# Spread modulation steps and a written-out VectorE order in the product FFNs of a diffusion backbone

## The chip, the cores and the metric

The kernel runs on one core of a Trainium2 chip. Five engines of that core take part: TensorE (PE) multiplies matrices into PSUM banks; VectorE (DVE) and ScalarE (ACT) do the element-wise work; GpSimd (POOL) and SyncE (SP) issue DMA transfers. Each engine works through its own list of instructions in order; semaphores tie the lists together. The metric is the device time of one execution in microseconds (us), the median of several runs.

## The reference, cut to what matters

The model is a trunk of two layers over 512 latent tokens and 256 context tokens, 1024 wide, in fp32. Each layer is a half-step SwiGLU FFN, a mixer (a gated convolution in layer 0, attention in layer 1), and a second half-step FFN. Each sub-layer has its own modulation vectors (shift, scale and gate), computed from a conditioning vector:

```python
for i in range(DEPTH):
    m_lat = (silu_c @ ada_w[i] + ada_b[i]).reshape(b, N_SUBLAYERS, N_MOD, 1, d)
    m_ctx = (silu_cc @ ada_w[i] + ada_b[i]).reshape(N_SUBLAYERS, N_MOD, 1, d)
    h = norm_modulate(x_lat, norm_g[i, 0], m_lat[:, 0, 0], m_lat[:, 0, 1])
    x_lat = x_lat + MACARON_WEIGHT * m_lat[:, 0, 2] * swiglu(h, ffn_w_in[i, 0], ffn_w_out[i, 0])
    ...                                # the same for the context, then the mixer, then the second FFN

def swiglu(h, w_in, w_out):
    gate, up = jnp.split(h @ w_in, 2, axis=-1)
    return (jax.nn.silu(gate) * up) @ w_out
```

## The kernel before, in words

**Stages.** The four sub-layers of layer 0 and 1 that matter here are called f00 (first FFN), c01 (the convolution), f02 (second FFN) and f10 (first FFN of layer 1); attention and the last FFN follow. All values are fp32. PE takes them as pairs: a high part (ACT copies the number into the rounded type, names ending in h or plain gh, tT3h, w) and a low part (DVE subtracts the high part from the number, names ending in l). One block of a product is then three matmuls: lines 808, 809 and 810. The helper `split` issues the copy (line 179) and the subtraction (line 180).

**Products.** The input half of an FFN (1024 to 2 x 2816) is computed in 22 chunks c of 128 gate and 128 up columns. Apart from two or three first chunks, which are multiplied plainly ("direct"), each chunk is done with seven products M1 to M7 in place of eight, on sums of token halves (T1 to T4, made once a stage) and sums of weight blocks (S1 to S4, made on DVE from the loaded `raw` tiles, lines 347 and 356). A product is 12 matmuls of 128x384. Their order on PE is M1(c), M2(c), M7(c-1), M5(c), M6(c), M4(c-1), M3(c-1). M1, M6, M7 and M4 of a chunk add up in one PSUM bank, ps_A; M5 and M3 in another, ps_C; M2 is in ps_B. In between, the partial results are read out of the bank, and the next product may not write to it until that has been done:

- M1: ACT copies ps_A to g (line 1067); M2: DVE adds ps_B to it (1069).
- M5: ACT copies ps_C to c (line 1072); M6: ACT copies ps_A to a second g (1075).
- M7: DVE adds ps_A to c (line 1078). M4 writes the same bank, and waits for it.
- M4: DVE multiplies ps_A into the silu of g (line 1129). M3: DVE adds ps_C to the second g (line 1083), which gives c12; its silu and a product with c follow (lines 1134 and 1137).

Every four chunks (28 products, a "T block") an "out" phase multiplies what the gate gave with the output weights: 144 matmuls of 512 or 256 columns into ps_A and ps_C, whose results DVE adds to the tokens x (line 874). It begins right behind M3, so its second ps_C bank is the one that line 1083 has to empty.

**Weights.** SP loads `raw` tiles (512 KB) into five buffers. `w_fill` turns them into `w` tiles (eight buffers), sums first, then high and low parts. At a stage's end some weights of the next stage are made ahead ("held").

**Modulation.** The vectors of later sub-layers are computed on DVE while PE multiplies. A block loads a 128x512 tile `aw` of ada_w (256 KB, by POOL, line 495) and reduces it against the silu of the conditioning row `crow`, once for the latents and, where they are needed, once for the context (line 505: a reduce that writes `jk` or back to `aw`, and a short read of the accumulator). `ADA_BY` says how far each stage gets: f00 computes 6 vectors (192 reduces), f02 4 (128), f10 5 (96). `bg()`, called after each product, hands out as many as are due, none in the out phases.

**What sets the order.** SP's and PE's lists are in program order. DVE's and ACT's lists are set by a scheduler that goes by its own estimates; a modulation reduce may be moved anywhere that its data allow, apart from the first of a stage.

Of the kernel before, what the change touches and what calls it, by code (L numbers as in the profile page):

```python
# [38 lines left out]
ADA_BY = {"f00": 6, "f02": 10, "f10": 15}  # L39
ADA_DEPTH = {"f00": 3, "f02": 3, "f10": 3}  # L40
# [80 lines left out]
def backbone(ctx: ExitStack, tc: tile.TileContext, a: dict, out: bass.AP):  # L121
# [56 lines left out]
    def split(dsth, dstl, src):  # L178
        act.activation(dsth, src, AF.Copy)  # L179
        dve.tensor_tensor(out=dstl, in0=src, in1=dsth.bitcast(F32), op=ALU.subtract)  # L180
# [64 lines left out]
    def w_fill(most=1 << 30):  # L245

        end = state["next"] + most
        while state["next"] < min(len(stream), end):
            n = state["next"]
            event, where, k, make = stream[n]  # L250
# [6 lines left out]
            raw_fill()  # L257
            dst = place(n, where, k)
# [8 lines left out]

    def w_get(most=1 << 30):
        w_fill(max(most, state["used"] + 1 - state["next"]))
# [17 lines left out]
    def add_plain(raw, u, ks, where=None, event=None):  # L287
        def make(dh, dl):
            split(dh, dl, raw_tiles[raw][0][:, u, ks])
            raw_used(raw)  # L290
        stream.append((event, where, ks.stop - ks.start, make))
# [50 lines left out]
    def add_product(g, u, m):  # L342
# [6 lines left out]
        def make(dh, dl):  # L349
            if m == "M1":  # L350
                split(dh, dl, quad(0))
            elif m == "M2":
                split(dh, dl, quad(1))
            elif m == "M5":
                sub(0, 0, 2)
                dve.tensor_tensor(out=quad(2), in0=quad(2), in1=quad(3), op=ALU.add)
                split(dh, dl, quad(2))
            elif m == "M6":
                sub(2, 3, 0)
                split(dh, dl, quad(2))  # L360
            elif m == "M7":
                split(dh, dl, quad(0))
            elif m == "M4":
                split(dh, dl, quad(3))
            else:
                sub(1, 1, 2)
                split(dh, dl, quad(1))
# [3 lines left out]
        stream.append((None, None, 4, make))  # L371
# [118 lines left out]
    def ada_next(n):  # L490

        if n < ahead["limit"]:
            i, m, k, c0 = ada_blocks[n]
            w = ada_loaded[n] = ahead["pool"].tile([P, HALF], F32, name=f"aw{i}_{m}_{k}_{c0}", tag="aw", bufs=ADA_DEPTH[ahead["key"]])
            nc.gpsimd.dma_start(w, a["ada_t"][i, m, k, :, c0 : c0 + HALF])  # L495

    def ada_block(n, v, nv):

        i, m, k, c0 = ada_blocks[n]
# [4 lines left out]
        if pinned[0]:  # L506
            tc.keep_in_program_order(ins)
        pinned[0] = False
        if v == nv - 1:
            ada_loaded.pop(n)  # L510
            ada_next(n + ADA_DEPTH[ahead["key"]])
# [13 lines left out]
    pinned = [False]  # L525
# [20 lines left out]
    def bg_start(key, pool, first, last):  # L546

        pace.update(n=0, done=0, first=first, last=last, tasks=ada_tasks.pop(key, []))
        pace["steps"] = len(pace["tasks"])
# [4 lines left out]
    def bg():  # L554
# [4 lines left out]
        if pace["n"] == pace["first"] - 6:  # L559
            rows_load(0)  # L560
# [1240 lines left out]
```

## Time and profile before

| what | value |
|---|---|
| time, median of 3 runs (lowest, highest) | 2502.87 us (2501.15, 2503.94) |
| time of the profiled execution | 2499.04 us |
| its span | 2497.3 us |
| mean granted clock of PE | 0.994 |
| f00, c01, f02, f10 begin at | 32, 584.8, 836.4, 1352.8 us |
| attention, last FFN begin at | about 1877, 2107 us |
| f02: out phase 0, first T block behind it | 875.22 to 891.90, 891.90 to 955.26 us |

The span is the time from the first to the last instruction; 1.7 us of the profiled execution lie outside it. The profiled execution is 3.8 us faster than the median of the runs. In the profile's parts, "busy" of PE counts overlapping matmuls once, and a matmul's duration is longer than the distance to the next one, since they are pipelined: 0.34 us long, one every 0.176 us, for 384 columns. DVE's durations too overlap a little: back-to-back subtractions of 128x512 last 0.69 us and start 0.60 us apart.

### The profile page before, as it was taken

How to read it: one execution, taken by the hardware profiler on the slowest of the kernel's cores; microseconds unless marked ns; L12 is line 12 of the kernel's file. 1: busy time of each engine (PE TensorE's matmuls, PEld its weight loads, DVE VectorE, ACT ScalarE, POOL GpSimd, SP SyncE). 2: the span in 40 equal slices, each digit the busy share in tenths (PEclk: the TensorE clock that was granted, in tenths of full speed). 3: DMA queues.
4: the chain of work that ended last, by engine and by line, in shares of the span. 5: the costliest groups of instructions: out<-in, count | busy, mean ns of one | idle time of the engine just before them, and what ended most of it. 6: DMA issues, size and time to landing. Idle time of an engine off the chain costs nothing.

```text
span 2497.3 us, 35662 instructions
## 1 busy us (share of the span) xinstructions
PE 2436.3 (98%) x13632; PEld 2263.3 (91%) x13632; DVE 1897.2 (76%) x3758; ACT 1094.2 (44%) x2016; POOL 135.1 (5%) x254
## 2 busy tenths in 40 slices
PE   6999999999999999999999999999999999999998
PEld 3889999999999999999999999899997889888887
DVE  4699999878968899996667989866668887544443
ACT  4443343355525643433435534244346775433233
POOL 0011111000000001110000021200000000000000
PEclk9999999999999999999999999999999999999999
DMA  7333543330213034533221155522231101332221
GB/s 276 110 125 116 165 155 129 110 110 26 76 51 117 28 106 148 161 123 102 85 74 49 67 172 167 183 79 68 68 110 60 43 18 60 102 101 93 96 82 34
DMA packets 92155, 252.53 MB, mean 101 GB/s; under 512 B 10192, under 2 KB 19536, under 8 KB 91984
## 3 DMA queue, kind: packets, MB, share of 16 engines
q1 hardware_dynamic: 71072, 183.00, 22.3%
q0 software_dynamic: 20064, 66.08, 8.2%
q8 instruction: 107, 1.75, 0.3%
q10 hardware_dynamic: 848, 1.18, 0.1%
q14 instruction: 64, 0.52, 0.1%
HBM read 248.11 MB, written 2.10 MB: 100 GB/s over the span
## 4 chain that ended last, share of the span: by engine, by line
PE 74%; issue 11%; DVE 8%; ACT 2%; POOL 2%; DMA 2%; SPq 0%; POOLq 0%; DVEq 0%; ACTq 0%
PE ps_A L809 14%; PE ps_A L808 14%; PE ps_A L810 14%; PE ps_C L808 7%; PE ps_C L810 7%; PE ps_C L809 7%; POOL aw L495 2%; PE ps_B L810 2%; PE ps_B L809 2%; PE ps_B L808 2%; DVE w L180 2%; DVE aw L505 1%; DVE jk L505 1%; PE ps_T L1481 1%; DVE x L874 0%
## 5 line engine op out<-in xcount | busy, mean ns | idle before, releaser
L179 ACT ACTIVATE w<-raw 128x512 fp32r<-128x512 f32 (+2 forms) x810 | 491.5, 618 | 752.4 <-PE ps_A L810 460.3
L180 DVE TENSOR_TENSOR w<-raw,w 128x512 fp32r<-128x512 f32 (+2 forms) x810 | 541.2, 677 | 183.9 <-ACT w L179 175.2
L809 PE MATMUL ps_A<-gl,w 128*128 128x512 f32 (+2 forms) x624 | 212.6, 341 | 0.4 <-DVE gl L180 0.4
L808 PE MATMUL ps_A<-gh,w 128*128 128x512 f32 (+2 forms) x624 | 212.1, 340 | 0.1
L810 PE MATMUL ps_A<-gh,w 128*128 128x512 f32 (+2 forms) x624 | 212.0, 340 | 0.0
L495 POOL DMA_DIRECT2D aw<-in_ada_t x240 | 129.6, 540 | 1130.5 <-DVE mods L505 1109.6
L874 DVE SCALAR_TENSOR_TENSOR x<-ps_A,gat,x 128x512 f32<-128x512 f32 (+1 forms) x192 | 118.6, 619 | 79.7 <-PE ps_A L810 79.5
L808 PE MATMUL ps_C<-gh,w 128*128 128x512 f32 (+1 forms) x472 | 166.6, 353 | 9.1 <-DVE g L1083 8.8
L809 PE MATMUL ps_C<-gl,w 128*128 128x512 f32 (+1 forms) x472 | 165.9, 352 | 0.0
L810 PE MATMUL ps_C<-gh,w 128*128 128x512 f32 (+1 forms) x472 | 165.7, 351 | 0.0
L809 PE MATMUL ps_A<-hl,w 128*128 128x512 f32 (+1 forms) x424 | 162.6, 384 | 2.4 <-DVE hl L668 2.4
L808 PE MATMUL ps_A<-h,w 128*128 128x512 f32 (+1 forms) x424 | 162.2, 382 | 1.0 <-DVE x L874 1.0
L810 PE MATMUL ps_A<-h,w 128*128 128x512 f32 (+1 forms) x424 | 162.1, 382 | 0.0
L347 DVE TENSOR_TENSOR raw<-raw,raw 128x512 f32<-128x512 f32 x204 | 139.5, 687 | 8.8 <-DMA raw<-in_ffn_w_in 6.3
L809 PEld LDWEIGHTS ps_A<-gl,w 128*128 128x128 f32 x624 | 118.6, 190 | 16.0 <-DVE gl L180 1.9
L808 PEld LDWEIGHTS ps_A<-gh,w 128*128 128x128 f32 x624 | 118.5, 190 | 15.2 <-ACT gh L179 1.0
L810 PEld LDWEIGHTS ps_A<-gh,w 128*128 128x128 f32 x624 | 118.6, 190 | 12.9
L874 DVE SCALAR_TENSOR_TENSOR x<-ps_C,gat,x 128x512 f32<-128x512 f32 (+1 forms) x136 | 87.7, 645 | 52.0 <-PE ps_C L810 51.8
L808 PEld LDWEIGHTS ps_C<-gh,w 128*128 128x128 f32 x472 | 90.0, 191 | 22.5 <-issue 11.3
L808 PE MATMUL ps_A<-tB11h,w 128*128 128x384 f32 x312 | 106.9, 343 | 3.0 <-ACT tB11h L763 2.9
L809 PE MATMUL ps_A<-tB11l,w 128*128 128x384 f32 x312 | 106.1, 340 | 0.3 <-DVE tB11l L765 0.3
L810 PE MATMUL ps_A<-tB11h,w 128*128 128x384 f32 x312 | 105.7, 339 | 0.0
(426 smaller groups left out, 6623.9 us busy)
## 6 DMA issues: line engine op xcount, KB each, us to landing
raw<-in_ffn_w_in SPq DMA_DIRECT2D x174, 512.0 KB, 3.7
aw<-in_ada_t POOLq DMA_DIRECT2D x240, 256.0 KB, 3.2
raw<-in_ffn_w_out SPq DMA_DIRECT2D x76, 512.0 KB, 3.9
raw<-in_conv_w_in SPq DMA_DIRECT2D x24, 512.0 KB, 3.7
ada<-in_ada_w SPq DMA_DIRECT2D x27, 256.0 KB, 6.0
raw<-in_attn_w_qkv SPq DMA_DIRECT2D x12, 512.0 KB, 4.8
raw<-in_ada_w SPq DMA_DIRECT2D x8, 512.0 KB, 5.2
raw<-in_conv_w_out SPq DMA_DIRECT2D x8, 512.0 KB, 3.7
```

Of the source, the lines that this page charges most:

```text
L179: act.activation(dsth, src, AF.Copy)
L180: dve.tensor_tensor(out=dstl, in0=src, in1=dsth.bitcast(F32), op=ALU.subtract)
L347: dve.tensor_tensor(out=quad(o), in0=quad(x), in1=quad(y), op=ALU.subtract)
L495: nc.gpsimd.dma_start(w, a["ada_t"][i, m, k, :, c0 : c0 + HALF])
L505: ins = dve.tensor_tensor_reduce(out=junk, in0=w, in1=ahead["rows"][:, v], scale=1.0, scalar=out if c0 else ada_b[:, i, m, k : k + 1], op0 ...
L808: pe.matmul(ps, wh, xh, start=first, stop=False, **kw)
L809: pe.matmul(ps, wh, xl, start=False, stop=False, **kw)
L810: pe.matmul(ps, wl, xh, start=False, stop=last, **kw)
L874: dve.scalar_tensor_tensor(out=x, in0=p[:, o - off : o - off + w], scalar=gat[:, m, v : v + 1], in1=x, op0=ALU.mult, op1=ALU.add)
L1481: pe.transpose(pt[:, c, :], pr[:, (c0 + c) * P : (c0 + c + 1) * P], ident)
```

## The change

- **The modulation is dealt out otherwise.** f00 computes 5 vectors (160 reduces), c01 one (32 reduces); f02 and f10 the same as before. Steps are due after each product (weight 1) and also inside the out phases (weights 6 and 3 in turn, 27 in all). Every reduce is held at its place in the program. In c01 the `aw` tiles have two buffers, elsewhere three.
- **The `aw` loads are issued by SP** instead of POOL, at the next call of `bg()` after their buffer came free.
- **DVE's order is written out** from the last direct chunk to the last out phase of f00, f02 and f10 (`chain()`, `unchain()`): what the program says first is first on DVE. A product's reading of PSUM comes first, then the modulation due, then the low parts that were put off (`late_parts`, emptied by `flush`), then the sums for the next weight (`pre()`). In the chain `w_get` makes only the weight that is needed, and `w_fill` runs after a product. ACT's order remains the scheduler's.

What is computed and PE's order of matmuls are the same; the number of reduces in all too (416). Line numbers move: 179 and 180 become 209 and 205 (the helper), 347 and 356 become 392 and 403, 505 becomes 554, 874 becomes 920, 1067 to 1083 become 1126 (copy of M1), 1128 (sum of M2), 1131 (copy of M5), 1134 (copy of M6), 1137 (sum of M7) and 1142 (sum of M3); 1129 and 1137 of before become 1202 and 1213.

```diff
-ADA_BY = {"f00": 6, "f02": 10, "f10": 15}
-ADA_DEPTH = {"f00": 3, "f02": 3, "f10": 3}
+ADA_BY = {"f00": 5, "c01": 6, "f02": 10, "f10": 15}
+ADA_DEPTH = {"f00": 3, "c01": 2, "f02": 3, "f10": 3}
+OUT_WEIGHT = (6, 3)
...
+    def chain():
+        chained.append(ExitStack())
+        chained[0].enter_context(tc.manual_schedule(engines=CHAIN_ORDERED))
+        w_fill()
...
+    def flush():
+
+        for _ in range(len(late_parts)):
+            late_parts.pop(0)()
+        if chained:
+            raw_fill()
...
-    def split(dsth, dstl, src):
+    def split(dsth, dstl, src, then=None):
+
+        def low():
+            dve.tensor_tensor(out=dstl, in0=src, in1=dsth.bitcast(F32), op=ALU.subtract)
+            if then:
+                then()
+
         act.activation(dsth, src, AF.Copy)
-        dve.tensor_tensor(out=dstl, in0=src, in1=dsth.bitcast(F32), op=ALU.subtract)
+        if chained:
+            late_parts.append(low)
+        else:
+            low()
...
+    def w_ahead():
+
+        flush()
+        if state["next"] < len(stream):
+            pre, raw = stream[state["next"]][4:]
+            if all(r in raw_tiles for r in raw):
+                pre()
+
     def w_get(most=1 << 30):
-        w_fill(max(most, state["used"] + 1 - state["next"]))
+        flush()
+        w_fill(max(0 if chained else most, state["used"] + 1 - state["next"]))
+        flush()
...
-            nc.gpsimd.dma_start(w, a["ada_t"][i, m, k, :, c0 : c0 + HALF])
+            nc.sync.dma_start(w, a["ada_t"][i, m, k, :, c0 : c0 + HALF])
...
-        if pinned[0]:
-            tc.keep_in_program_order(ins)
-        pinned[0] = False
+        tc.keep_in_program_order(ins)
...
-            ada_next(n + ADA_DEPTH[ahead["key"]])
+            ada_freed.append(n + ADA_DEPTH[ahead["key"]])
...
+    def bg(at):
+
+        while ada_freed:
+            ada_next(ada_freed.pop(0))
...
-        span = pace["last"] - pace["first"] + 1
-        due = min(pace["steps"], -(-pace["steps"] * (pace["n"] - pace["first"] + 1) // span))
+        pace["now"] += pace["slots"].get(at, 0)
+        due = min(pace["steps"], -(-pace["steps"] * pace["now"] // pace["total"]))
         while pace["done"] < due:
             pace["tasks"][pace["done"]]()
             pace["done"] += 1
...
+            if m == "out":
+                if begin <= count <= end:
+                    slots.update({(count, 1 + q): OUT_WEIGHT[q % 2] for q in range(6)})
...
             w_done()
             if c == total - 1:
                 traced.add((key, m))
+            if chained:
+                w_fill()
...
                 product(c, m)
-                bg()
+                traced_products += 1
+                bg((traced_products, 0))
+                if chained:
+                    w_ahead()
...
             if n == steps[-1]:
                 free_order()
+                if key != "c01":
+                    chain()
```

**The end of a T block.** DVE's list at the end of f10's second T block, before (the trace has it from 1564 to 1574 us). L1129 is the product of M4, L1083 empties the ps_C bank of M3, L505 is a modulation reduce and its accumulator read, L180 a low part (w of a weight, gl of the gate's result):

```order
L180 TENSOR_TENSOR w_14784<-raw_14659,w_14784 128x512
L505 ISA aw_5_5_512_16045,mods_81<-aw_5_5_512_16045,crow_15126,mods_81 128x512
L505 ISA mods_81 128x1
L1129 TENSOR_TENSOR g_14543<-g_14543,ps_A 128x384
L180 TENSOR_TENSOR w_14807<-raw_14706,w_14807 128x512
L505 ISA aw_5_6_512_16073,mods_81<-aw_5_6_512_16073,crow_15126,mods_81 128x512
L505 ISA mods_81 128x1
L180 TENSOR_TENSOR gl_14339<-g_14543,gh_14337 128x384
L1083 TENSOR_TENSOR g_14626<-ps_C,g_14626 128x384
```

The changed kernel's DVE list at the same place, with the out phase's first evictions (L920) behind it:

```order
L1202 TENSOR_TENSOR g_14548<-g_14548,ps_A 128x384
L205 TENSOR_TENSOR w_14789<-raw_14696,w_14789 128x512
L205 TENSOR_TENSOR gl_14360<-g_14548,gh_14358 128x384
L1142 TENSOR_TENSOR g_14625<-ps_C,g_14625 128x384
L554 ISA aw_7_5_0_14714,mods_81<-aw_7_5_0_14714,crow_13413,packed 128x512
L554 ISA mods_81 128x1
L205 TENSOR_TENSOR w_14809<-raw_14696,w_14809 128x512
L1213 TENSOR_TENSOR g_14625<-g_14625,c_14607 128x384
L205 TENSOR_TENSOR gl_14360<-g_14625,gh_14358 128x384
L920 SCALAR_TENSOR_TENSOR x<-ps_C,gat,x 128x512
L920 SCALAR_TENSOR_TENSOR x<-ps_A,gat,x 128x512
```

The two reduces that stood between the product of M4 and the sum of M3, or just ahead of them, are gone from there; the one that is due after M3 stands behind its sum.

**The first T block of a stage, ACT.** In f02, just behind out phase 0, before: tT3h and tT4h are high parts of the token sums T3 and T4, the three PSUM copies are those of M5, M6 and the next chunk's M1, the rest are high parts of weights:

```order
L179 ACTIVATE tT3h<-fT_8157 128x768 x2
L179 ACTIVATE tT4h<-fT_8418 128x768
L179 ACTIVATE w_8320<-raw_7561 128x512
L179 ACTIVATE w_8324<-raw_8214 128x512
L179 ACTIVATE w_8375<-raw_8214 128x512
L179 ACTIVATE w_8378<-raw_7550 128x512
L179 ACTIVATE w_8381<-raw_8222 128x512
L1072 ACTIVATE c_8453<-ps_C 128x384
L1075 ACTIVATE g_8475<-ps_A 128x384
L1067 ACTIVATE g_8494<-ps_A 128x384
L179 ACTIVATE w_8434<-raw_8222 128x512
L179 ACTIVATE w_8438<-raw_7561 128x512
```

The same place in the changed kernel; c_8563 is the copy of the next chunk's M5:

```order
L1134 ACTIVATE g_8488<-ps_A 128x384
L209 ACTIVATE tT4h<-fT_8430 128x768
L1126 ACTIVATE g_8507<-ps_A 128x384
L209 ACTIVATE tT3h<-fT_8166 128x768 x2
L209 ACTIVATE tT4h<-fT_8430 128x768
L1131 ACTIVATE c_8563<-ps_C 128x384
L209 ACTIVATE w_8465<-raw_7559 128x512
L209 ACTIVATE w_8486<-raw_8275 128x512
L209 ACTIVATE w_8505<-raw_8275 128x512
L209 ACTIVATE w_8523<-raw_8231 128x512
```

tT3h went from ahead of the PSUM copies to behind the third of them, and the copy of the next M5 went ahead of four weights' high parts.

**The first T block of a stage, DVE.** The same place on DVE, before, up to the sum of M7 (L1078) that M4 waits for; tT4l is the low part of T4:

```order
L180 TENSOR_TENSOR tT3l<-fT_8157,tT3h 128x768 x2
L180 TENSOR_TENSOR tT4l<-fT_8418,tT4h 128x768 x2
L347 TENSOR_TENSOR raw_8222<-raw_8222,raw_8214 128x512
L347 TENSOR_TENSOR raw_7550<-raw_7550,raw_7561 128x512
L347 TENSOR_TENSOR raw_8214<-raw_8214,raw_8222 128x512
L180 TENSOR_TENSOR w_8434<-raw_8222,w_8434 128x512
L180 TENSOR_TENSOR w_8438<-raw_7561,w_8438 128x512
```

Three more weights' low parts (w_8455, w_8479, w_8497), the sum of M2, one more low part and L1078 follow. In the changed kernel, from the same low parts to the sum of M7 (now L1137):

```order
L205 TENSOR_TENSOR tT3l<-fT_8166,tT3h 128x768 x2
L205 TENSOR_TENSOR tT4l<-fT_8430,tT4h 128x768 x2
L205 TENSOR_TENSOR w_8458<-raw_8233,w_8458 128x512
L205 TENSOR_TENSOR w_8460<-raw_7570,w_8460 128x512
L392 TENSOR_TENSOR raw_7559<-raw_7559,raw_7570 128x512
L205 TENSOR_TENSOR w_8465<-raw_7559,w_8465 128x512
L205 TENSOR_TENSOR w_8486<-raw_8275,w_8486 128x512
L205 TENSOR_TENSOR w_8505<-raw_8275,w_8505 128x512
L1128 TENSOR_TENSOR g_8507<-ps_B,g_8507 128x384
L205 TENSOR_TENSOR w_8523<-raw_8231,w_8523 128x512
L392 TENSOR_TENSOR raw_8275<-raw_8275,raw_8470 128x512
L403 TENSOR_TENSOR raw_8470<-raw_8470 128x512
```

The next row is L1137. DVE's number of instructions up to the sum is about the same; but the low part of w_8465 now has, ahead of its own high part on ACT, the copy of the next chunk's M5. The lists of f00 and f10 have the same rows at their first T block.

More of the change, by code (lines that the diff above doesn't have):

```diff
@@ L249, in w_fill @@
             n = state["next"]
-            event, where, k, make = stream[n]
+            event, where, k, make, pre, raw = stream[n]
             if event is not None and event not in traced:
@@ L257, in w_fill @@
             raw_fill()
+            if not all(r in raw_tiles for r in raw):
+                flush()
+            pre()
             dst = place(n, where, k)
@@ L288, in make @@
         def make(dh, dl):
-            split(dh, dl, raw_tiles[raw][0][:, u, ks])
-            raw_used(raw)
-        stream.append((event, where, ks.stop - ks.start, make))
+            split(dh, dl, raw_tiles[raw][0][:, u, ks], lambda: raw_used(raw))
+        stream.append((event, where, ks.stop - ks.start, make, lambda: None, (raw,)))
     def add_units(src, extra=None, event=None):
@@ L493, in ada_next @@
             i, m, k, c0 = ada_blocks[n]
-            w = ada_loaded[n] = ahead["pool"].tile([P, HALF], F32, name=f"aw{i}_{m}_{k}_{c0}", tag="aw", bufs=ADA_DEPTH[ahead["key"]])
-            nc.gpsimd.dma_start(w, a["ada_t"][i, m, k, :, c0 : c0 + HALF])
+            pool, tag = (tmp, "r") if ahead["key"] == "c01" else (ahead["pool"], "aw")
+            w = ada_loaded[n] = pool.tile([P, HALF], F32, name=f"aw{i}_{m}_{k}_{c0}", tag=tag, bufs=ADA_DEPTH[ahead["key"]])
+            nc.sync.dma_start(w, a["ada_t"][i, m, k, :, c0 : c0 + HALF])
     def ada_block(n, v, nv):
+        while n not in ada_loaded:
+            ada_next(ada_freed.pop(0))
         i, m, k, c0 = ada_blocks[n]
@@ L523, in rest @@
         pass
[L525 removed]
+    ada_freed = []
     pace = {}
@@ L544, in ada_list, with bg_start @@
             t0 = t1
-    def bg_start(key, pool, first, last):
-        pace.update(n=0, done=0, first=first, last=last, tasks=ada_tasks.pop(key, []))
-        pace["steps"] = len(pace["tasks"])
-        if pace["steps"]:
+    def bg_start(key, pool, slots):
+        tasks = ada_tasks.pop(key, [])
+        pace.update(tasks=tasks, steps=len(tasks), done=0, now=0, slots=slots, total=sum(slots.values()))
+        if tasks:
             ahead.update(pool=pool, key=key, start=ada_range[key][0], limit=ada_range[key][1])
-        pinned[0] = True
-    def bg():
-        pace["n"] += 1
+    def bg(at):
+        while ada_freed:
+            ada_next(ada_freed.pop(0))
         if not pace["steps"]:
             return
-        if pace["n"] == pace["first"] - 6:
+        first = min(pace["slots"])
+        if at == (first[0] - 6, 0):
             rows_load(0)
-        if pace["n"] == pace["first"] - 2:
+        if at == (first[0] - 2, 0):
             rows_silu()
@@ L1020, in products @@
         pairs = [0]
-        bg_start(key, stage["aw"], 10 if key == "c01" else 12, 7 * (total - 2 - direct) - 1)
+        begin, end = 10 if key == "c01" else 12, 7 * (total - 2 - direct) - 1
+        slots, count = {}, 0
+        for c, m in order:
+            if m == "out":
+                if begin <= count <= end:
+                    slots.update({(count, 1 + q): OUT_WEIGHT[q % 2] for q in range(6)})
+            elif c >= direct:
+                count += 1
+                if begin <= count <= end:
+                    slots[count, 0] = 1
+        bg_start(key, stage["aw"], slots)
+        traced_products = 0
         def directly(n, c, m):
@@ L1090, in products @@
                 last = c == len(parts) - 1
+                flush_all()
+                if last:
+                    unchain()
                 if last and isinstance(after, dict):
@@ L1093, in products @@
                 else:
-                    out_phase(BOTH, passes, *out_args(c), after if last else None, out_banks, 3)
+                    steps_of = out_steps(BOTH, passes, *out_args(c), after if last else None, out_banks, 3)
+                    for q, _ in enumerate(steps_of):
+                        if chained:
+                            w_fill()
+                        bg((traced_products, 1 + q))
+                        if chained:
+                            w_ahead()
                     if n in hooks:
```

51 lines of the change are left out of this document (32 added, 19 removed).

## The prediction

> **What bounds the kernel now.** I read the page's busy shares and its chain first, then PE's waits, and then, block by block, the windows of the three product FFNs.
>
> ```profile
> PE 2436.3 (98%) x13632; PEld 2263.3 (91%) x13632; DVE 1897.2 (76%) x3758; ACT 1094.2 (44%) x2016; POOL 135.1 (5%) x254
> PE 74%; issue 11%; DVE 8%; ACT 2%; POOL 2%; DMA 2%; SPq 0%; POOLq 0%; DVEq 0%; ACTq 0%
> PE ps_C L808 <- DVE g L1083: 8.8, 5, 3.8
> PE ps_A L808 <- DVE c L1078: 4.7, 2, 3.6
> ```
>
> The first line gives busy time: PE is the bound, and its matmuls stay as they are. So the change can only win what PE waits, and only what it waits for VectorE in these FFNs; the waits on boot and attention are not touched. The last two lines (total, times, longest) name it: PE waits for the sum of M3 at five block ends, and for the sum of M7, ahead of M4, twice.
>
> The waits' total leaves out matmuls that run slowly after a wait, so I take whole blocks. The columns are the stretch, its length, then busy time and count of PE, PEld, DVE, ACT and POOL, the granted clock, and DMA:
>
> ```profile
> 130.33:184.15 53.82, 50.21 (x279) 49.89 (x277) 50.84 (x108) 25.82 (x50) 5.93 (x11) 0.97 0.39 128
> 184.15:221.53 37.38, 35.20 (x194) 30.58 (x194) 34.65 (x79) 6.42 (x11) 6.47 (x12) 0.95 0.40 126
> 221.53:280.66 59.13, 59.13 (x338) 59.13 (x337) 58.64 (x133) 29.62 (x54) 8.64 (x16) 1.00 0.48 156
> 373.49:407.49 34.00, 33.61 (x193) 29.45 (x193) 33.66 (x80) 6.12 (x11) 5.98 (x12) 1.00 0.41 137
> 1048.10:1083.05 34.95, 33.61 (x193) 29.44 (x193) 34.47 (x81) 6.41 (x11) 6.46 (x12) 1.00 0.41 136
> 1471.68:1506.78 35.10, 33.84 (x194) 29.50 (x193) 30.57 (x70) 6.42 (x11) 10.70 (x20) 1.00 0.57 183
> 1506.78:1567.53 60.75, 59.68 (x338) 59.07 (x337) 54.44 (x120) 28.03 (x54) 11.62 (x22) 1.00 0.54 177
> 1567.53:1606.52 38.99, 35.20 (x193) 30.58 (x193) 33.13 (x75) 6.41 (x11) 11.31 (x21) 0.96 0.57 183
> 1665.66:1699.00 33.34, 33.34 (x194) 29.53 (x194) 18.05 (x30) 6.08 (x10) 0.00 (x0) 1.00 0.11 36
> ```
>
> A clean out phase lasts 33.34 us (last row, no modulation left), a clean T block of 28 products 59.13 us (third row), 2.112 us a product; f00's first T block has 23 products, clean 48.57 us. What each row has over that is the most that the change can win: f00 5.25 + 4.04 + 0.66, f02 1.61, f10 1.76 + 1.62 + 5.65, in sum **20.6 us**, 0.8% of the time. In f00's full T block DVE is busy 58.64 of 59.13 us: it has no room, and a sum that is due at the block's end comes late.
>
> The three long waits look like this on PE (start, duration, and in brackets the idle time before):
>
> ```profile
> 174.50 0.34 PE L810 MATMUL ps_A<-tT2h,w 128*128 128x384 f32 x1
> 178.45 0.69 PE L808 MATMUL ps_A<-tT4h,w 128*128 128x384 f32 x1 [3.61 <-DVE c L1078]
> 179.26 0.52 PE L810 MATMUL ps_A<-tT4h,w 128*128 128x384 f32 x1
> 179.58 0.52 PE L808 MATMUL ps_A<-tT4h,w 128*128 128x384 f32 x1
> 185.31 0.39 PE L810 MATMUL ps_A<-gh,w 128*128 128x512 f32 x1
> 187.87 0.47 PE L808 MATMUL ps_C<-gh,w 128*128 128x512 f32 x1 [2.18 <-DVE g L1083]
> 189.32 0.63 PE L809 MATMUL ps_C<-gl,w 128*128 128x512 f32 x1
> 189.75 0.63 PE L810 MATMUL ps_C<-gh,w 128*128 128x512 f32 x1
> 1572.86 0.47 PE L808 MATMUL ps_C<-gh,w 128*128 128x512 f32 x1 [3.79 <-DVE g L1083]
> 1568.00 0.75 DVE L505 CUSTOM_DVE_ANT_0 aw<-aw,crow,mods 128x512 f32<-128x512 f32 x1 [1.48 <-DMA aw<-in_ada_t]
> ```
>
> After each of them the matmuls are for a while almost twice as far apart (0.32 us for 384 columns against 0.176; 0.43 us for 512 against 0.23), which is the granted clock of 0.95 to 0.97 in their windows. That is in the 20.6: f00's first block lost 3.78 us waiting (174.50 to 178.45, less the 0.176 that one matmul takes) and 1.47 after it; f00's first out phase 2.33 and 1.7; f10's 3.95 and 1.7. The last row shows where f10's long wait comes from: DVE itself waits for a modulation tile, with the sum of M3 queued behind.
>
> **What the change removes.** At the block's end the sum of M3 (L1142) now has no modulation between it and the product of M4, two low parts at most. The modulation rows that stood there take 0.75 us each, and could wait for their tile on top (9.7 us idle in this group, 9.1 of it for the loads):
>
> ```profile
> L505 DVE CUSTOM_DVE_ANT_0 aw<-aw,crow,mods 128x512 f32<-128x512 f32 x120 | 89.2, 746 | 9.7 <-DMA aw<-in_ada_t 9.1
> ```
>
> The out phase needs the bank after six matmuls, 1.4 us by the distances of 0.23; the sum takes 0.55 (the duration of the same sum of M7, below), and is there 0.65 to 1 us behind M3. Nor is DVE saturated any longer: without modulation a T block holds 28 low parts and 16 sums of weights at 0.60 us, and 28 sums, products and low parts of 384 columns at 0.47, in all 39.7 us. f00's 160 reduces, 0.67 us apart, and 13 steps without work, over some 220 weighted places, make 0.8 steps a product: 22 in a T block, 15 us, so 55 of 59 us; f02 has 52, f10 49. I take all **20.6 us** away. Were only the three long waits gone, it would be 14.9.
>
> **What it adds, first of all at three places.** The first T block behind out phase 0, in f02 in the trace of before (E = 891.90 is the end of out phase 0):
>
> ```profile
> 894.73 1.81 DVE L180 TENSOR_TENSOR tT3l<-fT,tT3h 128x768 fp32r<-128x768 f32 x2
> 900.01 3.08 DVE L180 TENSOR_TENSOR w<-raw,w 128x512 fp32r<-128x512 f32 x5
> 904.09 0.55 DVE L1078 TENSOR_TENSOR c<-ps_A,c 128x384 f32<-128x384 f32 x1
> 884.76 1.58 ACT L179 ACTIVATE tT3h<-fT 128x768 fp32r<-128x768 f32 x2 [1.09 <-DVE fT L768]
> 898.43 0.50 ACT L1067 ACTIVATE g<-ps_A 128x384 f32<-128x384 f32 x1 [1.61 <-PE ps_A L810]
> 898.98 3.24 ACT L179 ACTIVATE w<-raw 128x512 fp32r<-128x512 f32 x6
> 904.77 0.49 ACT L1072 ACTIVATE c<-ps_C 128x384 f32<-128x384 f32 x1 [0.64 <-PE ps_C L810]
> 906.69 0.34 PE L808 MATMUL ps_A<-tT4h,w 128*128 128x384 f32 x1
> ```
>
> M4 starts at E+14.79, and the sum of M7 is done at E+12.74: nothing waits. In the changed kernel ACT's list has tT3h behind the copy of the next M1, which cannot start before E+6.53 (898.43), so tT3l starts at about E+7.9 instead of E+2.83. Then comes the copy of the next M5, not before E+12.87 (904.77), and only behind it the high part of w_8465, ready at E+13.9 (0.4 for the copy, 0.63 for the high part, which is longer than the 0.54 from one to the next). DVE, with w_8465 at the head of its list, does nothing until then. From there seven more instructions go to L1137: three low parts and two sums at 0.60, two PSUM sums at 0.47 of which the last counts 0.55 to its end, and w_8465 itself 0.60. That is 4.6 us, by E+18.6: **3.8 us** behind the time at which M4 could start, and nothing else can be multiplied meanwhile, since PE's list is in order. The rows are the same in f00 and f10. By the rows at 174.50 and 1572.86, waits of this length, some 1.5 us of slow matmuls follow: 5.3 us a place. The low end is 3.8, where the clock is kept; the high end 5.65, the row of f10. Three places: **15.9 us**. M7 just ahead waits about 0.2 us for tT3l: 0.6.
>
> The rule of the Trainium skill that bears on this ("TensorE: Matmul & The Clock Gate", part 1) is that the clock halves only after about one idle window of 3.4 us, which runs freely and isn't reset by work. A wait of 3.8 us would cover a whole such window about one time in eight, so by that rule the three places would cost some 12 us and not 16. The trace speaks against it as it stands: the wait of 2.33 us at 185.31 was followed by half speed too. I keep the rows.
>
> **Smaller terms.** At a stage's end ACT's copy of the last chunk's M6 stands behind three held high parts (0.54 us each by the row of six above), in f10 behind two more, and M7 waits for it: estimated at 0.2 + 0.2 + 1.3, **1.7 us** (0 where those are early, 4 where a raw tile for attention is late). f00's later chunks have the sum of M7 with little slack, 0.5 us (0 to 3). c01 gets 32 reduces of 0.67 us, 21.5 us on top of
>
> ```profile
> 605.00:625.00 20.00, 20.00 (x115) 19.75 (x114) 18.10 (x36) 10.30 (x17) 0.00 (x0) 1.00 0.09 27
> ```
>
> a stretch in which DVE has 10% left; over the whole stage, 252 us, that is 8.5% more. PE does not wait for DVE there now; I take 0, and 3 as the bound. The 240 loads on SP stand in its list behind the raw loads that were due; three buffers last for several products, more than the 1.48 us of the row above: 0, and up to 5 if they hold back raw tiles.
>
> **The sum.** The profiled execution took 2499.04 us: span 2497.3 and 1.7 around. 2499.04 - 20.6 + 15.9 + 0.6 + 1.7 + 0.5 = 2497.1. The runs' median is 3.8 us above that execution, which I add: **2501.0 us**, 1.9 us or 0.1% below the median of before. The waits move from block ends to the first T blocks.
>
> **The rivals.** A difference under 0.2%, 5 us, is about what a measurement of this kernel cannot tell from none.
>
> - **The clock holds** after the new waits: 3.8 a place, 11.4 us, which gives 2496.5. By the rule of the Trainium skill named above it would come out much the same. For it: the granted clock is 1.00 in the windows with losses of 1.6 to 1.8 us. Against it: it is 0.95 to 0.97 in all three with a wait over 2 us. Chance 0.17.
> - **No new wait:** DVE comes to L1137 in time, because its steps overlap more than the rows say. Then only the small terms remain: 2501.0 - 16.5 = 2484.5. Against it: the high part of w_8465 can't come before E+13.9, and M4 wants its bank at E+14.79; eight instructions in 0.9 us aren't in any row. Chance 0.10.
> - **Slower: SP's queue.** An aw load can be issued only when the reduce that frees its tile is done, and the raw loads behind it in SP's list are held as long. In f00 DVE has 4.3 us to spare in a T block (59.13 less 55), with 11 loads in it (two reduces each), so it decides from 0.4 us of delay a load. At 0.7 us, five blocks would lose 5 x 11 x 0.3, 16 us: 2517. For it: DVE has waited for these very loads, 9.1 us in the group above, when POOL issued them. Against it: the raw loads behind them mostly wait for DVE's rows in the same order. Chance 0.20.
> - **It doesn't do what it says:** the block ends stay late, since the low parts ahead of the sum wait for ACT: half of the 20.6 stays, 2511. Chance 0.05.
>
> **How the numbers follow.** The forecast has 0.48, by its own bounds 2497 to 2508 (down by 1.5 for two clocks and 1 for the stage ends, up by 2.3 for those and 5 for f00's chunks and c01). The range from 2489 to 2512 takes in these, the kept clock and the milder half of the slower cases, and leaves out the case without a new wait. Faster by over 0.2% (under 2497.9): the kept clock mostly, no new wait, and a little of the forecast, 0.30. Slower (over 2507.9): SP's queue, the late block ends, a little of the forecast, 0.23. Within: 0.47.
>
> **What would show it.** PE's waits for the sum of M3 should be gone from the list; waits of ps_A for L1137 should be there three times with some 3.7 us each, the first at about 145 us, with DVE idle ahead of them for ACT w L209. The out phases should last 33.4 us. If instead the clock is 1.00 in those three windows, the clock holds; if DVE waits there for a DMA of raw, it is SP's queue. A wait at another place that no row of before has would make the prediction wrong.

## The result, and the profile after

| kernel | median, us (lowest, highest) | ratio to before, 95% interval |
|---|---|---|
| before | 2502.01 (2499.62, 2503.94) | |
| changed | 2542.55 (2539.49, 2543.92) | 1.0161 (1.0143 to 1.0178) |

The change makes the kernel 40 us slower; the range ended at 2512. The profiled execution has a span of 2541.4 us, 44.1 more than before.

PE's waits in the changed kernel (total, times, longest):

```profile
PE ps_A L854 <- DVE c L1137: 26.2, 14, 3.8
PE ps_A L854 <- DVE x L920: 12.9, 12, 2.3
PE ps_A L854 <- ACT g L1134: 5.1, 2, 2.6
```

The waits for the sum of M3, 8.8 us before, are gone from the list. In their place stand three others: for the sum of M7 (L1137), 14 times and not three; for the evictions of the out phases (L920), 12 times; and for ACT's copy of M6 (L1134), twice.

The same blocks as before, with the same columns (stretch, length, busy time and count of PE, PEld, DVE, ACT and POOL, granted clock, DMA): a T block and two out phases that were long before, then the blocks that are long now.

```profile
186.00:220.55 34.55, 33.62 (x194) 29.45 (x194) 26.12 (x58) 4.70 (x8) 0.00 (x0) 1.00 0.27 85
1554.16:1613.29 59.13, 59.13 (x338) 59.13 (x337) 51.76 (x105) 29.77 (x57) 0.00 (x0) 1.00 0.53 169
1613.29:1646.63 33.34, 33.34 (x193) 29.53 (x193) 22.11 (x47) 4.65 (x8) 0.00 (x0) 1.00 0.33 105
892.96:915.19 22.23, 18.82 (x97) 15.86 (x97) 16.04 (x29) 4.07 (x8) 0.00 (x0) 0.92 0.25 82
915.19:985.41 70.22, 66.24 (x362) 65.60 (x361) 58.72 (x109) 34.75 (x64) 0.00 (x0) 0.95 0.37 117
414.79:478.86 64.07, 60.95 (x339) 60.30 (x338) 59.35 (x128) 30.34 (x57) 0.00 (x0) 0.97 0.43 138
1018.75:1078.98 60.23, 59.40 (x338) 59.08 (x337) 55.23 (x117) 29.76 (x57) 0.00 (x0) 1.00 0.45 143
```

f10's long out phase is down from 38.99 to 33.34 us, f00's from 37.38 to 34.55. But out phase 0 of f02 (fourth row) lasts 22.23 us for 16.68, its first T block 70.22 for 63.36, and f00's later T blocks 63 to 64 us for 59.13, although DVE has about as much to do in them as before (59.35 us busy in 64.07; before, 58.64 in 59.13).

Summed over the blocks of f00, f02 and f10 by kind, from the first matmul of each to the first of the next (the last kind runs up to the next stage's first out phase; of f10 it has the last T block alone):

| kind of block | clean | before | changed |
|---|---|---|---|
| out phase 0, three | 50.1 | 50.1 | 61.9 |
| first T block, three | 175.3 | 180.5 | 194.1 |
| later full T blocks, nine | 532.2 | 534.0 | 549.2 |
| later out phases, twelve | 400.1 | 414.5 | 405.7 |
| last T block and stage end, three | 363.0 | 363.0 | 375.3 |

Before, the blocks had 21.4 us over clean; none of those waits is left. Now they have 65.5 us over clean, all of it new: 11.8 + 18.8 + 17.0 + 5.6 + 12.3. The difference is the 44.1 us of the spans.

### The profile page after: what moved, and what is told of

Read it like the earlier page. It is cut to its first block, busy times and chain, and to the rows that moved or that the text cites. A ratio compares the mean times of both kernels' runs of the same rounds, so it can differ in the third digit from the quotient of the medians.

```text
span 2541.4 us, 35496 instructions
## 1 busy us (share of the span) xinstructions
PE 2453.1 (97%) x13632; PEld 2272.9 (89%) x13632; DVE 1898.4 (75%) x3758; ACT 1093.6 (43%) x2018; POOL 7.1 (0%) x16
## 4 chain that ended last, share of the span: by engine, by line
PE 81%; DVE 12%; ACT 3%; issue 2%; DMA 1%; SPq 0%; DVEq 0%; ACTq 0%
PE ps_A L854 16%; PE ps_A L855 16%; PE ps_A L856 15%; PE ps_C L854 8%; PE ps_C L855 7%; PE ps_C L856 7%; DVE w L205 3%; PE ps_B L855 2%; PE ps_B L856 2%; PE ps_B L854 2%; DVE jk L554 1%; DVE x L920 1%; DVE raw L392 1%; DVE aw L554 1%; DVE raw L403 1%
## 5 line engine op out<-in xcount | busy, mean ns | idle before, releaser
L209 ACT ACTIVATE w<-raw 128x512 fp32r<-128x512 f32 (+2 forms) x810 | 485.7, 619 | 893.4 <-PE ps_A L856 332.5
L854 PE MATMUL ps_A<-gh,w 128*128 128x512 f32 (+2 forms) x624 | 213.4, 342 | 12.3 <-DVE x L920 11.9
L920 DVE SCALAR_TENSOR_TENSOR x<-ps_A,gat,x 128x512 f32<-128x512 f32 (+1 forms) x192 | 118.6, 620 | 85.1 <-PE ps_A L856 85.0
L920 DVE SCALAR_TENSOR_TENSOR x<-ps_C,gat,x 128x512 f32<-128x512 f32 (+1 forms) x136 | 87.7, 645 | 89.4 <-PE ps_C L856 89.0
L392 DVE TENSOR_TENSOR raw<-raw,raw 128x512 f32<-128x512 f32 x204 | 140.1, 687 | 4.6 <-DMA raw<-in_ffn_w_in 2.4
L854 PE MATMUL ps_A<-tT4h,w 128*128 128x384 f32 x272 | 96.7, 356 | 26.2 <-DVE c L1137 26.2
L854 PE MATMUL ps_C<-tB22h,w 128*128 128x384 f32 x296 | 101.8, 344 | 0.0
```

The costliest lines, as they stand in the source:

```text
L392: dve.tensor_tensor(out=quad(o), in0=quad(x), in1=quad(y), op=ALU.subtract)
L854: pe.matmul(ps, wh, xh, start=first, stop=False, **kw)
L920: dve.scalar_tensor_tensor(out=x, in0=p[:, o - off : o - off + w], scalar=gat[:, m, v : v + 1], in1=x, op0=ALU.mult, op1=ALU.add)
```

## The experiments

Each ran beside the kernel before on one chip; the times are medians, the ratios are to that kernel. Four questions: is it the written order; which of its places; is it DVE's load or the order; and what, in the part that remains, makes the gain.

**The written order taken away.**

```diff
                 free_order()
-                if key != "c01":
-                    chain()
```

> The changed kernel without the written-out order (chain() is never called): modulation is still spread, held in place and loaded by SP. Theory (the written order puts DVE's steps in the wrong place at three kinds of spots: out phase 0 and the first T block, the out phases, the first chunk behind them): the first-T-block waits for L1137 (18.8 us with their slow matmuls), out phase 0 (some 12 us) and most of the waits at later T blocks go, so the time falls from 2542 to 2495-2510. Rival (SP's queue holds raw tiles back, or the spread modulation by itself is the load): the waits stay, 2530 or more.

Measured 2477.85 us, ratio 0.9898 (0.9881 to 0.9914): 24 us faster than before, 65 faster than the changed kernel. The windows of f00's first T block, an out phase and a later T block, then f02's out phase 0 and first T block in this kernel:

```profile
129.32:177.90 48.58, 48.58 (x279) 48.58 (x277) 44.34 (x85) 26.69 (x51) 0.00 (x0) 1.00 0.41 132
177.90:211.26 33.36, 33.36 (x194) 29.53 (x194) 28.36 (x64) 6.00 (x10) 0.00 (x0) 1.00 0.28 93
211.26:270.39 59.13, 59.13 (x338) 59.13 (x337) 55.35 (x122) 28.12 (x54) 0.00 (x0) 1.00 0.49 156
864.49:881.21 16.72, 16.72 (x98) 14.76 (x97) 16.45 (x30) 6.28 (x11) 0.00 (x0) 1.00 0.34 111
881.21:944.57 63.36, 63.36 (x362) 63.36 (x361) 56.11 (x107) 31.33 (x60) 0.00 (x0) 1.00 0.38 127
```

Every block is clean to 0.2 us, with the modulation spread and loaded just as in the changed kernel; DVE's 55.35 us in a T block of f00 are the 55 that the prediction worked out. So the change is a gain of 24 us and a loss of 65, and the whole loss is the written order's. It was expected to be less well off (2495 to 2510): the gain was underrated. Between the two profiled executions it is 20.0 us (spans of 2497.3 and 2477.3), which is what the blocks of before had over clean; the medians differ by 4 us more, since the profiled execution of before was a quick one.

**The written order begun behind out phase 0.**

```diff
                     behind_outs.clear()
+                    if c == 0 and key != "c01":
+                        chain()
...
-                if key != "c01":
-                    chain()
```

> The written order begins behind out phase 0 and the token sums T3 and T4, not ahead of them; all else as changed. Theory: out phase 0 is back at 16.7 us and the first T block at 63.4 us in f02 and f10 (the row of tT3h on ACT is ahead of the PSUM copies again), which takes some 28 to 30 us away: 2511-2516. The waits in the later T blocks of f00 and f02 stay (some 21 us), and so do those in the later out phases. Rival (the first T block waits because DVE has too much to do, whatever the order): the first T blocks keep 69 to 70 us and the time stays over 2530.

Measured 2514.42 us, ratio 1.0050 (1.0035 to 1.0065), within what was expected. f02's out phase 0 and first T block, and a later T block of f00:

```profile
885.04:901.72 16.68, 16.68 (x97) 14.75 (x97) 16.45 (x30) 6.29 (x11) 0.00 (x0) 1.00 0.34 111
901.72:965.85 64.13, 63.60 (x363) 63.31 (x362) 56.17 (x106) 31.85 (x60) 0.00 (x0) 1.00 0.40 127
213.53:276.41 62.88, 59.87 (x339) 58.93 (x338) 59.02 (x129) 29.84 (x57) 0.00 (x0) 1.00 0.45 143
```

Out phase 0 is clean again, the first T block loses 0.8 us and not 6.9, the later T blocks are as late as in the changed kernel. So some 28 us of the loss lie at the beginning of the written stretch.

**ACT in program order too.** DVE's list is that of the changed kernel, row by row.

```diff
-CHAIN_ORDERED = {mybir.EngineType.DVE}
+CHAIN_ORDERED = {mybir.EngineType.DVE, mybir.EngineType.Activation}
```

> As the changed kernel, with ACT's list in program order too within the written stretch; DVE's list is the same row by row. Theory (the first T block waits because the scheduler put ACT's copy of the next M5 and the high part of T3 elsewhere than DVE's written order needs them): L1137 is then due at about E+14.2, M4 at E+14.8, so the first T blocks fall from 69-70 to 63.4-64 us in f02 and f10 and by some 6 in f00, and the stage ends' waits for L1134 go: 2515-2526. Rival (DVE's written order alone makes them late): the first T blocks stay within 1 us of 70 and 69.

Measured 2542.57 us, ratio 1.0162 (1.0147 to 1.0177): no better, a miss. The first T blocks last 60.4, 73.0 and 72.2 us (changed: 54.6, 70.2, 69.3). The wait for L1137 did go from them; another came. The rows are of PE, of ACT and, last, of DVE in f02's first T block, which begins at 913.53:

```profile
929.04 0.69 PE L854 MATMUL ps_A<-tT3h,w 128*128 128x384 f32 x1 [6.90 <-ACT g L1134]
927.08 0.63 ACT L209 ACTIVATE w<-raw 128x512 fp32r<-128x512 f32 x1 [2.28 <-DVE raw L392]
927.62 0.47 ACT L1131 ACTIVATE c<-ps_C 128x384 f32<-128x384 f32 x1
928.51 0.48 ACT L1134 ACTIVATE g<-ps_A 128x384 f32<-128x384 f32 x1
921.60 1.83 DVE L205 TENSOR_TENSOR tT3l<-fT,tT3h 128x768 fp32r<-128x768 f32 x2 [0.97 <-ACT tT3h L209]
```

ACT's copies of M5 and M6 now stand behind a high part that waits for a sum of weights on DVE (L392), and DVE does that sum behind T3 and T4. tT3l starts 8.07 us into the block, no sooner than in the changed kernel (7.97). So ACT's order by itself isn't the cause: with either order of ACT, DVE's list has T3, T4 and weights where the sums of PSUM should come through. The equal times also hide that things moved. In the profiled execution f00's out phase 0 begins 7.1 us earlier than in the changed kernel's (105.39 for 112.51); behind it the first T blocks and out phases 0 take 14.5 us more, and the last T blocks with the stage ends 5.0 less: the waits for L1134 there did shrink, as expected.

**Less modulation, first in the out phases, then behind the products.** These two leave out about half of the modulation each.

```diff
-        ins = dve.tensor_tensor_reduce(out=junk, in0=w, in1=ahead["rows"][:, v], scale=1.0,
+        wide = 8 if pace["at"][1] else HALF
+        ins = dve.tensor_tensor_reduce(out=junk[:, :wide], in0=w[:, :wide], in1=ahead["rows"][:, v, :wide], scale=1.0,
...
     def bg(at):
+        pace["at"] = at
```

The second run has `8 if not pace["at"][1] else HALF`.

> Each modulation reduce that is due inside an out phase reads 8 columns in place of 512, at the same place in the order (the modulation vectors are incomplete: this leaves out about half of that work). Theory (the bursts of reduces among the evictions hold up the evictions, and what is behind them on DVE at the start of the T block): the waits for L920 in the later out phases (some 5 us) and for L1137 in the first chunk of the later T blocks (some 21 us in f00 and f02) go; first T blocks and out phase 0 stay: 2514-2520. Rival (the T block's own load is what makes its first chunk late): only the 5 us go, 2535 to 2538.

> The counterpart of the run with cheap reduces in the out phases: reduces due after a product read 8 columns, those in the out phases all 512 (about half of the modulation is left out). Theory (the burst in the out phase is what makes the first chunk of a later T block late): the waits of f00's and f02's later T blocks for L1137 stay for the most part, 60.5 to 63 us a block, and the time is 2530-2541. Rival (the T block's own modulation makes its first chunk late): the later T blocks come down to 59.2, and the time to 2514-2520.

Measured 2517.41 us (ratio 1.0058, 1.0043 to 1.0073) and 2530.04 us (1.0110, 1.0094 to 1.0125). With cheap reduces in the out phases, a later out phase and T block of f00, and f02's first T block:

```profile
185.72:219.06 33.34, 33.34 (x194) 29.54 (x194) 18.97 (x62) 4.69 (x8) 0.00 (x0) 1.00 0.28 89
404.12:463.25 59.13, 59.13 (x338) 59.13 (x337) 55.35 (x123) 29.51 (x57) 0.00 (x0) 1.00 0.48 151
895.32:965.47 70.15, 66.16 (x363) 65.53 (x362) 58.73 (x109) 34.77 (x64) 0.00 (x0) 0.95 0.36 117
```

Later out phases and T blocks are clean, but for one T block of f02 (60.4 us), with the T blocks' own modulation in place (55.35 us of DVE); what happens at the first T block stays. With cheap reduces behind the products instead, f00's later T blocks still last 60.5 to 60.9 us. So the burst in the out phase is what is needed for the wait; with the T block's own load what is lost more than doubles (blocks of 62.9 to 64.1 us in the changed kernel).

**The reduces ahead of a step's evictions**, with the written order from behind out phase 0 as above; and then the last T block left to the scheduler.

```diff
             if gates:
                 gates.pop()()
+            while ahead_of_evictions:
+                ahead_of_evictions.pop()()
             for m, p in zip(ms, ps):
...
+                    if c == len(parts) - 2 and chained:
+                        unchain()
```

The list holds the call of `bg()` that is due in this step. The last two lines are in the second run only.

> The written order from behind out phase 0 (2514.4), and in the out phases the reduces stand ahead of a step's evictions, in the time of its matmuls, not behind them. Theory (a burst between one step's evictions and the next weights is what makes evictions and the next T block late): the out phases come to 33.4 us and f00's and f02's later T blocks to 59.2-60, some 20 to 24 us less: 2490-2496. Rival (the place of the burst does not matter, only its amount): 2508 or more.

> As the kernel with reduces ahead of evictions, and the written order ends behind the last out phase but one, so that the last T block is the scheduler's. Theory (ACT's copy L1134 at a stage's end stands behind held weights that wait for DVE's written order): the last T blocks of f02 and f10 are clean, some 8 to 11 us less: 2479-2487. Rival (the held weights make it late in any order): as the kernel before it, within 2 us.

Measured 2493.50 us (ratio 0.9966, 0.9954 to 0.9978) and 2484.59 us (0.9933, 0.9918 to 0.9948), both times as expected. With the same reduces, only elsewhere in the list, an out phase of f00 and the T blocks behind it and behind f02's:

```profile
179.49:212.81 33.32, 33.32 (x193) 29.53 (x193) 28.66 (x66) 4.22 (x7) 0.00 (x0) 1.00 0.35 114
212.81:273.95 61.14, 59.82 (x339) 58.89 (x337) 56.71 (x120) 30.18 (x57) 0.00 (x0) 1.00 0.42 139
988.50:1047.64 59.14, 59.14 (x339) 59.14 (x337) 53.26 (x109) 29.81 (x57) 0.00 (x0) 1.00 0.42 138
```

The out phases are clean, f02's T blocks too but for 0.5 us in one; f00's, expected at 59.2 to 60, keep 2 to 2.6 us each of the 3.7 to 3.9 that they lost with the burst behind the evictions. What holds these up was not tested. In the second run the last T block and stage end of f00, f02 and f10 together take 363.0 us, the clean value, for 370.6 in the first. What is left over clean blocks lies in f00's later T blocks (6 us in all) and the first ones (2.3 us).

**What makes the gain.** Four kernels without the written order: the loads by POOL; f00 with its six vectors of before; no steps in the out phases; and reduces that the scheduler may move.

```diff
-            nc.sync.dma_start(w, a["ada_t"][i, m, k, :, c0 : c0 + HALF])
+            nc.gpsimd.dma_start(w, a["ada_t"][i, m, k, :, c0 : c0 + HALF])
...
-ADA_BY = {"f00": 5, "c01": 6, "f02": 10, "f10": 15}
+ADA_BY = {"f00": 6, "f02": 10, "f10": 15}
...
-OUT_WEIGHT = (6, 3)
+OUT_WEIGHT = (0, 0)
...
-        tc.keep_in_program_order(ins)
+        if pinned[0]:
+            tc.keep_in_program_order(ins)
+        pinned[0] = False
```

> No written order, aw loads issued by POOL; all else as in the kernel without the written order (2477.9). Theory (the queue matters little): 2477-2481. Rival (SP's queue brings the gain): 2490 or more.

> No written order, and the division of before: f00 computes six vectors, c01 none. All else as in the kernel without the written order (2477.9). Theory (the spreading into the out phases is what relieves the T blocks, c01's share is a margin only: 0.96 steps a product make 58 of 59 us of DVE in f00's T blocks): 2478-2484. Rival (taking a vector out of f00 is a large part of the gain): 2488 or more.

> No written order, and no modulation due in the out phases (weights 0 and 0), so all of it follows products, as before the change; still held in place, still loaded by SP, c01 still has its share. Theory (of the 25 us that the kernel without the written order wins, the spreading into the out phases brings most, since DVE's T blocks in f00 are full without it): 2495 or more. Rival (holding the reduces in place, or SP's queue, brings it, and the spreading nothing): 2476-2481.

> No written order, and the reduces are free to be moved by the scheduler again (only the first of a stage is held); spread as in the changed kernel. Theory (spreading in the program is of no use if the scheduler may pull the reduces ahead into the T blocks, as it did before): the block-end waits come back in part, 2488 or more. Rival (the program's places are enough): 2476-2481.

Measured 2479.81 (0.9910, 0.9894 to 0.9925), 2480.54 (0.9913, 0.9897 to 0.9930), 2511.49 (1.0035, 1.0023 to 1.0048) and 2484.78 us (0.9933, 0.9918 to 0.9948). The queue and c01's share cannot be told from nothing (their intervals overlap with that of 0.9898). Without steps in the out phases the kernel is 34 us slower, slower than before even, and PE waits 10.7 us for the sum of M3 again: the gain needs the steps there. Free reduces cost 7 us, between what was expected of the two theories, so the steps in the out phases bring 17 us without being held in place, and holding them the rest. In the kernel with free reduces PE waits again for two of the sums of M3 and three evictions (its line numbers are four higher: L1146 is the sum of M3, L924 the eviction):

```profile
PE ps_A L858 <- DVE x L924: 4.7, 3, 2.0
PE ps_C L858 <- DVE g L1146: 2.3, 2, 1.7
```

**POOL in the changed kernel.** The same edit of the queue with the written order in place:

> The aw loads are issued by POOL again, still at the next call of bg(); all else as changed. Theory: the issuing queue does not matter, 2540-2545. Rival (SP's queue holds raw tiles back behind aw loads): the waits for L1137 shrink, 2525 or less.

Measured 2551.82 us, ratio 1.0197 (1.0182 to 1.0212): 9 us slower than the changed kernel, where no difference was expected. The rival, that SP's queue makes it slow, falls. Its profiled execution shows DVE waiting 2.1 us for the loads, and T blocks longer by up to 2.4 us; why 9 us come of it wasn't tried and stays open.

## Why the prediction was wrong

From one profiled execution to the other 1.9 us less were forecast, and 44.3 more were measured: 46.2 us apart. Forecast and median are 41.6 apart only because the 3.8 us added for them did not recur: the changed kernel's profiled execution took 2543.31 us, 0.8 more than its median. That was luck.

**What bounds the kernel, and what is removed: right.** PE is the bound, and the waits for the sum of M3 are gone in the changed kernel; no other in which the modulation is spread and held in place has more than one, of 1.4 us at most. The kernel without the written order shows the gain by itself: its blocks are clean, and it is 20 us faster by the profiled executions, 24 by the medians, where 20.6 were summed.

**The first T blocks: right in place and size, half right in the mechanism.** M4 waits for L1137 at 146.4, 930.2 and 1466.6 us, 4.0, 3.9 and 3.9 us (from one matmul's start to the next, less the 0.176 that it takes; predicted 3.8), and the three blocks lose 6.0, 6.9 and 5.9 us, 18.8 in all, with slow matmuls and M7's wait for tT3l (predicted 15.9 + 0.6). The rows of DVE in f02, then of ACT and PE, E being 915.19 here:

```profile
920.19 1.81 DVE L814 TENSOR_TENSOR fT<-f,f 128x768 f32<-128x768 f32 x2
923.16 1.83 DVE L205 TENSOR_TENSOR tT3l<-fT,tT3h 128x768 fp32r<-128x768 f32 x2 [1.15 <-ACT tT3h L209]
927.84 0.69 DVE L392 TENSOR_TENSOR raw<-raw,raw 128x512 f32<-128x512 f32 x1
929.55 1.90 DVE L205 TENSOR_TENSOR w<-raw,w 128x512 fp32r<-128x512 f32 x3 [1.02 <-ACT w L209]
933.76 0.55 DVE L1137 TENSOR_TENSOR c<-ps_A,c 128x384 f32<-128x384 f32 x1
928.51 0.49 ACT L1131 ACTIVATE c<-ps_C 128x384 f32<-128x384 f32 x1 [3.92 <-PE ps_C L856]
934.36 0.69 PE L854 MATMUL ps_A<-tT4h,w 128*128 128x384 f32 x1 [3.79 <-DVE c L1137]
```

tT3l starts at E+7.97 (predicted 7.9), the three low parts wait for ACT until E+14.36, and the sum ends at E+19.1 (predicted 18.6).

That the times agree so well is partly luck. The prediction put them down to ACT's list: tT3h behind the copy of M1, and the high part of w_8465 behind the copy of the next M5. But DVE idles for ACT only 1.15 and 1.02 us there; the rest is its own list. fT, from which tT3h is made, begins at E+5.00, behind the out phase's last evictions; before, it began 8.2 us ahead of E (883.72). And the high part of w_8465 is made from a sum of weights (L392) that ends at E+13.34, when M5's copy has just begun (E+13.32): without the copy ahead of it, it would come some 0.4 us earlier, an estimate from the distance of ACT's rows. The run with ACT in program order bears this out: tT3l starts no sooner there. What the prediction overlooked is that the written order puts fT, T3 and T4, some 5 us of DVE, behind the evictions and ahead of the sums; begun behind them, it costs f02's block 0.8 us and not 6.9.

**The step that failed first: "f00's later chunks have the sum of M7 with little slack, 0.5 us (0 to 3)".** That term measured 17.0 us in the full T blocks (12.5 in f00, 4.4 in f02, none in f10), and a part of the 12.3 of the last ones. What stands behind it is in DVE's list at the end of f00's first long out phase (PE's T block begins at 220.55):

```profile
219.87 0.74 DVE L554 CUSTOM_DVE_ANT_0 jk<-aw,crow,packed 128x512 bf16<-128x512 f32 x1
...
222.81 0.75 DVE L554 CUSTOM_DVE_ANT_0 jk<-aw,crow,packed 128x512 bf16<-128x512 f32 x1
223.48 1.29 DVE L205 TENSOR_TENSOR w<-raw,w 128x512 fp32r<-128x512 f32 x2
224.69 0.69 DVE L392 TENSOR_TENSOR raw<-raw,raw 128x512 f32<-128x512 f32 x1
225.29 0.48 DVE L920 SCALAR_TENSOR_TENSOR x<-ps_C,gat,x 128x256 f32<-128x256 f32 x1
...
231.64 0.69 DVE L392 TENSOR_TENSOR raw<-raw,raw 128x512 f32<-128x512 f32 x1
232.36 0.69 DVE L403 TENSOR_TENSOR raw<-raw 128x512 f32<-128x512 f32 x1
232.97 0.55 DVE L1137 TENSOR_TENSOR c<-ps_A,c 128x384 f32<-128x384 f32 x1
```

Five reduces (one step of weight 6) run from 219.87 to 223.48, and the out phase's last evictions come behind them, 4.7 us after PE had finished the phase. All weight work of the new T block comes later still, so DVE enters the block that much behind, with 55 of 59 us of work in it. The prediction averaged DVE's load over blocks (55 of 59) and asked whether it fits; with a list in order, the question is what stands ahead of the row that PE waits for. The runs with cheap reduces show that the burst is the cause, and the one with the reduces ahead of the evictions that its place is, for all but 0.5 us in f02. In f00, 7.0 of 11.3 us stay with the burst in the better place, and the cause of these stays open.

**A term that was missing: the evictions.** No step priced L920 in the out phases. A step's burst stands between two steps' evictions, and PE needs the banks back: 5.6 us over the later out phases. In out phase 0, which has no reduces, it is weights that stand ahead: DVE waits for a high part, ACT for that weight's transfer, and the evictions stand behind, with two more sums of weights ahead of them (L392 and L403, 1.4 us). In f02, DVE's rows, ACT's and PE's:

```profile
894.92 0.43 DVE L205 TENSOR_TENSOR w<-raw,w 128x256 fp32r<-128x256 f32 x1 [1.41 <-ACT w L209]
899.40 0.75 DVE L920 SCALAR_TENSOR_TENSOR x<-ps_C,gat,x 128x512 f32<-128x512 f32 x1
894.47 0.73 ACT L209 ACTIVATE w<-raw 128x256 fp32r<-128x256 f32 x2 [2.18 <-DMA raw<-in_ffn_w_out]
900.87 0.39 PE L854 MATMUL ps_A<-gh,w 128*128 128x256 f32 x1 [2.22 <-DVE x L920]
```

The first eviction is at 6.4 us of the phase (892.96); before, it was at 3.8 us. The three phases lose 11.8 us, which the run with the order begun behind out phase 0 gives back.

**The stage ends: right mechanism, too small.** Predicted 1.7 us (0 to 4). M7 of the last chunk waits 2.7 us for L1134 in f02 and in f10; the last blocks lose 12.3 us in all, first chunks and slow matmuls included. f00's, which has no wait for L1134, loses 4.3 of them. Left to the scheduler, they are clean. What ACT waits for there, ahead of L1134, is a raw tile of the next stage, in f02:

```profile
1345.45 0.63 ACT L209 ACTIVATE w<-raw 128x512 fp32r<-128x512 f32 x1 [2.09 <-DMA raw<-in_ffn_w_in]
1347.55 0.47 ACT L1134 ACTIVATE g<-ps_A 128x384 f32<-128x384 f32 x1
```

**The rivals.** SP's queue was the slower case, with 0.20; it did not happen: without the written order SP and POOL give the same, and with it POOL is the slower. The case on the slower side that did happen, bursts in an order that may not be changed, was not among them. (DVE's spare time in that rival is 4.1 us, 59.13 less 55, and the sum of a T block's steps 39.6; neither slip changes a figure that follows.)

## What to carry to other kernels

An order written out by hand takes away the scheduler's freedom to let a late eviction pass a long step; so for every row that the bound engine waits for, count what stands ahead of it in the list, not whether the block's load fits. Spread background work into stretches in which the engine idles, and put it ahead of the rows that wait for the end of the other engine's run, in their waiting time. A change with two parts is worth two measurements: here one part was 24 us of gain and the other 65 us of loss, and the kernel without the second, 2477.85 us, is the best of all; the best of the written orders tried, 2484.59 us, does not reach it.

## What the runs showed of the hardware

Whether slow matmuls follow a wait isn't set by its length alone. In f10's out phase 0 PE waits twice for L920, in the changed kernel and in the one with cheap reduces. The phase and its first wait in the changed kernel:

```profile
1430.83:1451.55 20.72, 17.19 (x98) 14.73 (x98) 16.09 (x29) 4.13 (x8) 0.00 (x0) 1.00 0.27 89
1438.84 0.39 PE L854 MATMUL ps_A<-gh,w 128*128 128x256 f32 x1 [2.33 <-DVE x L920]
```

and in the one with cheap reduces, whose line numbers are two higher:

```profile
1402.44:1424.59 22.15, 18.82 (x98) 15.86 (x97) 16.03 (x29) 4.07 (x8) 0.00 (x0) 0.92 0.24 82
1410.27 0.39 PE L856 MATMUL ps_A<-gh,w 128*128 128x256 f32 x1 [2.14 <-DVE x L922]
```

The granted clock is 1.00 behind the longer of the two and 0.92 behind the shorter, whose phase lasts 1.4 us more. What decides is where the wait falls. In each of the fourteen traces of this case the granted clock changes only on a grid of 3.41 us, whose phase differs from one execution to the next. The steps of that grid around the two waits, first the changed kernel's, then the other's (busy time of PE behind the comma, granted clock third from the end):

```profile
1434.59:1438.00 3.41, 1.92 (x15) 1.64 (x13) 3.26 (x7) 1.15 (x2) 0.00 (x0) 1.00 0.55 192
1438.00:1441.41 3.41, 2.57 (x14) 2.27 (x15) 2.78 (x7) 0.00 (x0) 0.00 (x0) 1.00 0.19 71
1407.69:1411.10 3.41, 1.27 (x11) 1.07 (x10) 3.26 (x7) 0.63 (x1) 0.00 (x0) 1.00 0.46 154
1411.10:1414.51 3.41, 3.41 (x11) 2.65 (x10) 1.60 (x4) 0.00 (x0) 0.00 (x0) 0.50 0.00 0
```

The grid cuts the longer wait in two: PE idles 1.49 us in one step and 0.84 in the next, and the clock stays. The shorter lies within one step, PE idles 2.14 us of it, and the clock is half for the next step. All steps at full clock between 100 us and attention, in all fourteen traces, divide this way: behind 1.91 us of idle time or more the clock is half in the next step, behind 1.86 or less it never is (both of these are from the changed kernel with POOL's loads, at 1125.67 and 231.37 us). So a wait of 3.8 us, of which the grid leaves at least 1.9 in one step wherever it cuts, almost surely brings slow matmuls, as all three in the first T blocks did; the rival in which the clock holds had next to no room. Shorter waits went either way: one of 1.97 us was followed by half clock (the changed kernel, 330.72), one of 2.51 us was not (cheap reduces in the out phases, 541.51). The rule of the Trainium skill that was weighed in the prediction has a window of 3.4 us that runs freely, which agrees with the 3.41 us here; that it takes a whole window of idle time does not, since 2.1 us of it were enough.
